# Buffers handed to the most urgent tile, and one layer's split weights kept in DRAM, in a two-layer hybrid decoder step

## The chip, the cores and the metric

One core of one Trainium2 chip runs the whole program. The metric is the device time of one execution in microseconds; lower is better. Three timed runs of the kernel before are known, and one profiled execution, from which all rows below come.

## The reference, cut to what matters

A prompt of 2048 tokens and a group of 8 samples with one new token each (and 2048 cached ones) go through two layers that share their weights. The even layer joins a gated MLP (A) and a stick-breaking attention (B); the odd one joins a top-k attention (C) and a pooling mixer (D). Each layer has one projection of its input and one of its output.

```python
def even_mixer(x, past_kv, w_in, w_sp, b_sp):          # layer 0
    h = jnp.einsum('btd,de->bte', x, w_in)
    u, v, gate_a, q, k, vb, gate_b = _split(h, EVEN_SPLITS)
...
    return jnp.concatenate([out_a, out_b], axis=-1), new_kv, v

def odd_mixer(x, past_kv, past_kidx, pool_buf, w_in, rel_bias, w_grp, scale):   # layer 1
    h = jnp.einsum('btd,de->bte', x, w_in)
    q, kv, q_idx, k_idx, w_idx, gate_c, p, gate_d = _split(h, ODD_SPLITS)
...
    return jnp.concatenate([out_c, out_d], axis=-1), new_kv, k_idx, new_buf

def post_norm(x, h, w_o, g, b):
    return _layer_norm(DN_ALPHA * x + jnp.einsum('bte,ed->btd', h, w_o), g, b)
```

All of it is float32. Layer 1's weights are `w_in_odd` (the projection of `odd_mixer`) and `w_out[1]`.

## The kernel before

**Tiling.** The prompt is cut into four blocks of 512 tokens. For each block and layer there are stages: `p0` (input projection of layer 0), `mixer_b`, `o0` (output projection of layer 0), `p1a` and `p1b` (input projection of layer 1), the tiles of mixer C (`c_tiles`: 16 query tiles of 128 tokens, with a top-k selection for each), and `o1`. The samples run as a stream beside them (`sample0`, `sample1`). The program interleaves up to three streams (`par`).

**Weights.** A projection multiplies in two parts: a value is split into a rounded part (`hi`, dtype float32r) and the rest (`lo`), and three products are added (xh·wh, xl·wh, xh·wl; lines 735 to 737, and 1132 to 1134 for the output projection). Weights come in pieces of 128 x 1024 numbers, 512 KB. `load_w` (line 656) brings each by a DMA on SP's queue into a tile `wr` (two buffers), ScalarE copies it into `wh` (line 661), and two VectorE subtractions of 512 columns make `wl` (line 664). `wh` and `wl` have two buffers each. Weights are read anew for every block: layer 1's input weights are 20 pieces, used by four blocks; its output weights are 8 pieces, used by four blocks, four of them once more for the last 128 rows (`out_tail`).

**Buffers.** SBUF tiles `tmp` (short-lived results) and `ot` (input and output of a block) have four buffers each; PSUM has two banks each of `pp` (projections), `pz` (the logits `z` of mixer B, `z_c` and `z_i` of C) and `pt` (transposes). VectorE or ScalarE must have read a bank before TensorE may fill it again.

**What sets the order.** The class `Order` plans each engine's instruction order before the program is built: `plan` goes through time with estimated costs, takes on each engine the ready instruction with the earliest latest-start (`latest`), and `settle` keeps the order with the shortest replay. `keep` fixes that order. In `plan`, tiles of one kind get their buffers strictly in the order in which the program names them (`queue[g].pop()` inside `take`), and the next one is served only after the first instruction of the one before it has started (`open_`).

**A branch in each selection.** `topk` ends with a check on VectorE and a conditional block (line 1595, `tc.If`); it is entered 14 times, and every engine's order is cut there.

Of the kernel before, what the change touches and what calls it, by code (L numbers as in the profile page):

```python
# [11 lines left out]
F32 = mybir.dt.float32  # L12
F32R = mybir.dt.float32r
# [9 lines left out]
P = 128  # L23
# [60 lines left out]


class Order:
# [4 lines left out]
    TILED, STAY, PATIENT = 150, 500, 40e3  # L91
    GUESSES = ((1.0, 200), (1.0, 250), (1.04, 230))
    ROUNDS, DRAWS, SPREAD = 5, 2, 0.05
# [48 lines left out]
    def gather(self):  # L142
# [83 lines left out]
        for t in sorted(self.uses, key=lambda t: self.uses[t][0]):  # L226
            if self.tiles[t].space != DRAM:
                self.tags.setdefault(self.tiles[t].tag, []).append(t)


# [86 lines left out]

    def settle(self):

        N, eng = len(self.ins), self.eng  # L320
        self.costs = [self.cost(n) for n in range(N)]
        for g, ms in self.group.items():
            busy = sum(self.costs[m][0] for m in ms)
            self.costs[g] = busy, busy + 170
        self.dma = [e is not None and "DMA" in i.opcode for e, i in zip(eng, self.ins)]
        self.kinds = [self.kind(n) for n in range(N)]
        self.ports = [self.port(n) for n in range(N)]
        self.succ = [[] for _ in range(N)]
        for n, d in enumerate(self.dep):
            for m in d:  # L330
                self.succ[m].append(n)
        self.links()
        draws, mid, best = [self.draw(k) for k in range(self.DRAWS)], self.costs, None
        sem = self.SEM
        for by, near in self.GUESSES:
            self.costs = [(b * by, l * by) if e in self.TAIL else (b, l) for e, (b, l) in zip(eng, mid)]
            self.SEM = near
            self.plan(list(range(N)))
            for _ in range(self.ROUNDS):
                self.SEM = near  # L340
                self.plan(self.latest())
                self.SEM = sem
                x = sum(self.replay(c) for c in draws)
                if best is None or x < best[0]:
                    best = x, self.order, self.after
        self.costs, (_, self.order, self.after) = mid, best

# [77 lines left out]
    def turns(self):  # L425
# [12 lines left out]
        return out  # L438

    def plan(self, rank):  # L440

# [9 lines left out]
        queue = {g: ts[::-1] for g, ts in self.tags.items()}  # L451
        free = {g: max(self.tiles[t].tag_meta.bufs for t in ts) for g, ts in self.tags.items()}
        open_ = dict.fromkeys(queue, True)
        users = {t: len(u) for t, u in self.uses.items()}
        self.after, gone = {}, {g: [] for g in queue}
        since, done, self.begun = [0.0] * N, [0.0] * N, [0.0] * N
# [11 lines left out]
        def take(g, t):  # L468
            while queue[g] and free[g] and open_[g]:
                x = queue[g].pop()  # L470
                if gone[g]:
                    self.after[x] = gone[g].pop(0)
                free[g] -= 1
                open_[g] = False
                for n in self.uses[x]:
                    release(n, t)
# [6 lines left out]
        while count < N:  # L483
            while back and back[0][0] <= now:
                _, g, x = pop(back)
                free[g] += 1
                gone[g].append(x)
                take(g, now)
# [9 lines left out]
            for e, q in ready.items():  # L498
                while q and idle[e] <= now:
# [42 lines left out]
                    for t in tiles[n]:  # L542
                        g, u = home[t], self.uses[t]
                        if n == u[0]:
                            open_[g] = True
# [67 lines left out]

    def keep(self):
        info = mybir.DependencyInfo(mybir.DependencyClass.NoSync, mybir.DependencyReason.DATA)
# [9 lines left out]
class Body:  # L625
    def __init__(self, ctx, tc, I, O):
        self.ctx, self.tc, self.nc, self.I, self.O = ctx, tc, tc.nc, I, O
        pool = lambda n, b, **k: ctx.enter_context(tc.tile_pool(name=n, bufs=b, **k))
        self.cst = pool("cst", 1)
# [25 lines left out]

    def load_w(self, src, shape, pool, bufs=2):
        nc = self.nc
        raw = self.loc.tile(shape, F32, tag="wr", name="wr", bufs=self.bufs["wr"])
        nc.sync.dma_start(raw, src)
        hi, lo = (pool.tile(shape, F32R, tag=n, name=n, bufs=bufs) for n in ("wh", "wl"))  # L660
        nc.scalar.copy(hi, raw)  # L661
        h = shape[1] // 2
        for e, c in ((nc.vector, slice(0, h)), (nc.vector, slice(h, 2 * h))):
            e.tensor_tensor(lo[:, c], raw[:, c], hi[:, c].bitcast(F32), op=OP.subtract)  # L664
        return hi, lo

    def rsqrt(self, out, var, eps, n):
# [9 lines left out]
        for _ in range(3):  # L677
# [3 lines left out]
            v.tensor_tensor(out, out, t[:n], op=OP.mult)  # L681

    def ps(self, name, shape=(P, TB)):

        b = next(b for b in BANKS.get(name, "pt").split() if b in self.banks)
        return self.banks[b].tile(list(shape), F32, tag=b, name=name)

    def tmp(self, name):
        return self.loc.tile([P, TB], F32, tag="tmp", name=name, bufs=self.bufs["tmp"])

# [124 lines left out]
    def plan_w(self, stages):  # L815

        I = self.I
        self.wplan, self.wready = [], []
        for st in stages:
            if st[:3] == "out":  # L820
                w = I["w_out"][int(st[3])]
                self.wplan += [(w[hf * 512:(hf + 1) * 512, cg * 256:(cg + 1) * 256], [P, 4, 256])
                               for cg in range(4) for hf in HALVES[int(st[3])]]
                continue
# [4 lines left out]
            w = I["w_in_even" if st == "p0" else "w_in_odd"][0]  # L829
            self.wplan += [(w[:, c:c + n], [P, KT, n]) for c, n in cols]  # L830
        for _ in range(2):
            self.more_w()

    def more_w(self, pool=None):
        if self.wplan:
            src, shape = self.wplan.pop(0)
            src = src.rearrange("(kt p) n -> p kt n", p=P)
            self.wready.append(self.load_w(src, shape, *((pool, 4) if pool else (self.wp,))))

# [247 lines left out]
    def otile(self, name):  # L1087
        return self.loc.tile([P, TB], F32, tag="ot", name=name, bufs=self.bufs["ot"])

# [1374 lines left out]

def build(nc, shapes):
    I = {n: nc.dram_tensor(n, s, d, kind="ExternalInput").ap() for n, s, d in shapes}
    O = {n: nc.dram_tensor("out_" + n, s, F32, kind="ExternalOutput").ap() for n, s in _OUTS}
    with tile.TileContext(nc, schedule_with_timeline_sim=True) as tc:
        with ExitStack() as ctx:
            body = Body(ctx, tc, I, O)  # L2470
            body.run()
        order = Order(tc, body.lags)
        order.gather()
        order.settle()
        order.keep()

# [12 lines left out]
```

## Time and profile before

| | us |
|---|---|
| median of 3 runs | 2790.44 |
| lowest, highest | 2785.44, 2792.58 |
| the profiled execution | 2784.49 |
| its span, first to last instruction | 2782.8 |
| TensorE busy in the span | 2672.8 |

The profiled execution took 1.7 us more than its span, and it is 6 us under the median. The profile lists, for each engine, the time in which an instruction of it was running. Matmuls overlap in TensorE's pipeline, and a running one that waits inside the pipeline counts as busy, so that TensorE's busy time holds stalls too; the distance from start to start tells them. PEld is TensorE's loading of its stationary operand. PEclk is the granted share of TensorE's clock.

### The profile page before, as it was taken

The page shows a single profiled execution, that of the slowest core. Times are in us where ns is not written, and L with a number is a line of the kernel's source. Part 1 is how long each engine was busy: PE and PEld are TensorE (multiplying, and loading weights), DVE is VectorE, ACT ScalarE, POOL GpSimd, SP SyncE. Part 2 cuts the span into 40 slices and gives each one's busy share as a digit, 9 for nine tenths or more (in the row PEclk, how much of TensorE's full clock was granted, in tenths as well). Part 3 has the DMA queues.
Part 4 walks back from the last instruction along what each step waited for, and adds up shares of the span by engine and source line. Part 5 has one row for each costly group of instructions (what it writes and reads, how often), then busy time and mean ns, then how long its engine had stood idle before and what let it go on. Part 6 is the DMA issues. An engine that isn't in the chain of part 4 may idle for free. (4 is left out here: it accounts for less than half of the span.)

```text
span 2782.8 us, 52464 instructions
## 1 busy us (share of the span) xinstructions
PE 2672.8 (96%) x17490; PEld 2154.5 (77%) x17490; DVE 2060.9 (74%) x5557; ACT 1604.3 (58%) x3216; POOL 766.3 (28%) x1040
## 2 busy tenths in 40 slices
PE   9999999999999999989899999999999999899996
PEld 7888787777777887768677677778777889898985
DVE  3466568775857886747988888897898788888865
ACT  3434333444444354435657677786686788688854
POOL 0111112210202321033433522334411445344222
PEclk9999999999999999999999999999999999999998
DMA  8666857895777777563764545433675666767462
GB/s 251 168 186 207 266 169 245 242 302 161 224 213 205 222 207 249 181 178 116 211 199 132 166 131 157 127 102 115 190 220 149 199 192 200 221 200 235 125 197 81
DMA packets 538914, 524.58 MB, mean 189 GB/s; under 512 B 43447, under 2 KB 411224, under 8 KB 538607
## 3 DMA queue, kind: packets, MB, share of 16 engines
q1 hardware_dynamic: 528759, 485.34, 58.9%
q0 software_dynamic: 9856, 35.66, 4.1%
q8 instruction: 139, 2.28, 0.3%
q14 instruction: 160, 1.31, 0.1%
HBM read 431.33 MB, written 89.73 MB: 187 GB/s over the span
## 5 line engine op out<-in xcount | busy, mean ns | idle before, releaser
L735 PE MATMUL pp<-xh,wh 128*128 128x512 f32 (+1 forms) x1536 | 624.0, 408 | 2.5 <-ACT wh L661 1.6
L736 PE MATMUL pp<-xl,wh 128*128 128x512 f32 (+1 forms) x1536 | 615.4, 401 | 0.0
L737 PE MATMUL pp<-xh,wl 128*128 128x512 f32 (+1 forms) x1536 | 613.6, 400 | 0.0
L664 DVE TENSOR_TENSOR wl<-wr,wh 128x512 fp32r<-128x512 f32 x520 | 354.5, 699 | 161.7 <-ACT wh L661 146.8
L661 ACT CAST wh<-wr 128x1024 fp32r<-128x1024 f32 x260 | 270.2, 1040 | 321.4 <-PE pp L736 160.2
L735 PEld LDWEIGHTS pp<-xh,wh 128*128 128x128 f32 (+1 forms) x1536 | 287.6, 188 | 67.4 <-issue 8.5
L737 PEld LDWEIGHTS pp<-xh,wl 128*128 128x128 f32 (+1 forms) x1536 | 287.6, 187 | 61.5 <-issue 4.4
L736 PEld LDWEIGHTS pp<-xl,wh 128*128 128x128 f32 (+1 forms) x1536 | 288.2, 188 | 53.9 <-issue 5.3
L1132 PE MATMUL pp_o<-wh,oh 128*128 128x256 f32 x1008 | 294.2, 294 | 5.4 <-DVE xres L1137 3.6
L1133 PE MATMUL pp_o<-wl,oh 128*128 128x256 f32 x1008 | 290.5, 289 | 0.2 <-DVE wl L664 0.2
L1134 PE MATMUL pp_o<-wh,ol 128*128 128x256 f32 x1008 | 288.5, 289 | 0.0
L1065 ACT COPY P<-ps_p 128x512 f32<-128x512 f32 (+2 forms) x320 | 166.5, 524 | 178.3 <-PE ps_p L1064 156.2
L1041 DVE TENSOR_TENSOR_SCAN P<-P,bfst 128x512 f32<-128x512 f32 x192 | 250.0, 1317 | 14.5 <-ACT P L1034 7.6
L1763 PE MATMUL z_c<-ksc,qc 128*128 128x512 f32 (+3 forms) x816 | 221.3, 356 | 22.9 <-DVE mx L1765 13.1
L1781 ACT ACTIVATE zt<-zt,nmax 128x512 f32<-128x512 f32 (+3 forms) x320 | 209.6, 657 | 54.1 <-DVE nmax L1769 52.2
L1750 POOL TENSOR_TENSOR nm<-nm,mk 128x256 f32<-128x256 f32 (+1 forms) x128 | 98.4, 770 | 420.2 <-DMA nm<-bft 161.3
L1796 ACT COPY zt<-ps_pc 128x512 f32<-128x512 f32 (+3 forms) x320 | 163.8, 522 | 81.6 <-PE ps_pc L1794 79.2
L1027 PE MATMUL z<-ks,q 128*128 128x512 f32 (+3 forms) x640 | 195.0, 390 | 13.1 <-DVE mx L1765 5.1
L1132 PEld LDWEIGHTS pp_o<-wh,oh 128*128 128x128 f32 x1008 | 193.3, 192 | 12.6 <-DVE xres L1137 4.6
L1133 PEld LDWEIGHTS pp_o<-wl,oh 128*128 128x128 f32 x1008 | 194.3, 193 | 4.1 <-issue 1.1
L1134 PEld LDWEIGHTS pp_o<-wh,ol 128*128 128x128 f32 x1008 | 193.4, 193 | 4.5 <-issue 2.2
L1509 ACT ACTIVATE mk<-ix,tk_tn 128x1152 int8<-128x1152 f32 (+13 forms) x140 | 183.8, 1313 | 17.7 <-DVE tk_tn L1559 6.6
(455 smaller groups left out, 5518.0 us busy)
## 6 DMA issues: line engine op xcount, KB each, us to landing
pg<-cache_b_kv SPq DMA_DIRECT2D x256, 256.0 KB
wr<-w_in_even SPq DMA_DIRECT2D x112, 512.0 KB
wr<-w_in_odd SPq DMA_DIRECT2D x76, 512.0 KB
wr<-w_out SPq DMA_DIRECT2D x68, 512.0 KB
ks<-ksc SPq DMA_DIRECT2D x80, 256.0 KB
ksc<-kcs SPq DMA_DIRECT2D x80, 256.0 KB
q<-qsc SPq DMA_DIRECT2D x64, 256.0 KB
qc<-qcs SPq DMA_DIRECT2D x128, 128.0 KB
```

The lines of the kernel that those rows point to most:

```text
L661: nc.scalar.copy(hi, raw)
L664: e.tensor_tensor(lo[:, c], raw[:, c], hi[:, c].bitcast(F32), op=OP.subtract)
L735: nc.tensor.matmul(ps[:m], wh[:, kt, :m], xh[kt], start=a, stop=False)
L736: nc.tensor.matmul(ps[:m], wh[:, kt, :m], xl[kt], start=False, stop=False)
L737: nc.tensor.matmul(ps[:m], wl[:, kt, :m], xh[kt], start=False, stop=b)
L1027: nc.tensor.matmul(z[:, :n], q2[:, c, t * P:(t + 1) * P].bitcast(F32R), ks[:, :n].bitcast(F32R), start=c == 0, stop=c == 1)
L1041: nc.vector.tensor_tensor_scan(r, r, r, initial=ini, op0=OP.mult, op1=OP.bypass)
L1132: nc.tensor.matmul(ps[:, :256], oh[:, tt], wh[:, k], start=a, stop=False)
L1133: nc.tensor.matmul(ps[:, :256], oh[:, tt], wl[:, k], start=False, stop=False)
L1134: nc.tensor.matmul(ps[:, :256], ol[:, tt], wh[:, k], start=False, stop=b)
L1763: nc.tensor.matmul(z[:, :n], q2[:, c, jj % 2, :].bitcast(F32R), kk, start=c == 0, stop=c == 1)
L1781: nc.scalar.activation(zt, zt, AF.Exp, bias=nmx, accum_out=st["rs"][:, h, c:c + 1])
```

## The change

It has two parts, and both alter the order that the planner writes.

**Buffers by urgency (`FREELY`).** For the kinds `ot`, `tmp`, `pt`, `pz` and `pp`, a free buffer goes to the most urgent waiting tile (by the planner's rank, among the first 8) instead of the next in program order, if `safe` finds that the tiles left can still be served in order. Which buffer each tile gets is planned too, so the kernel is built twice: the first build raises `Planned` with the order, the second takes the buffers from it (`turn`).

**Kept weights (`KEEP`).** For the first block in each of `p1a`, `p1b` and `out1`, the two parts `wh` and `wl` are written to DRAM after the split, 28 pieces in all, two DMAs each. For later blocks `load_w` reads both parts back, straight into `wh` and `wl`, with no ScalarE or VectorE work: 60 pieces of input weights and 28 of output weights. Every third of these (`THIRD`), outside `out_tail`, takes both buffers of `wr` in place of `wh` and `wl`.

```diff
+THIRD = True
+KEEP = {"p1a": 0, "p1b": 0, "out1": 0}
+FREELY = ('ot', 'tmp', 'pt', 'pz', 'pp')
...
+    def choose(self, queue, urgent, free, held, pending, any_):
+
+        least = queue[0]
+        if pending and (not any_ or self.span[pending][0] < self.span[least][0]):
+            return None
+        for x in urgent[:self.WINDOW] if any_ and not pending else ():
+            first = self.span[x][0]
+            if x != least and first > self.span[least][0] + self.AHEAD:
+                continue
+            for _, b in sorted(((held[b][0], b) for b in free if held[b][0] < first), reverse=True):
+                if self.safe(queue, held, x, b):
+                    return x, b
...
         def take(g, t):
-            while queue[g] and free[g] and open_[g]:
-                x = queue[g].pop()
...
+            while queue[g] and free[g]:
+                x = self.choose(queue[g], urgent[g], free[g], held[g], open_[g], g in self.free)
...
-    def load_w(self, src, shape, pool, bufs=2):
+    def load_w(self, src, shape, key, pool=None):
         nc = self.nc
-        raw = self.loc.tile(shape, F32, tag="wr", name="wr", bufs=self.bufs["wr"])
+        wr = lambda d, n: self.loc.tile(shape, d, tag="wr", name=n, bufs=self.bufs["wr"])
+        new = lambda d, n: (pool or self.wp).tile(shape, d, tag=n, name=n, bufs=4 if pool else 2)
+        kept = self.kept_w.get(key[::2])
+        if kept:
+            self.n_kept += 1
+            f = wr if THIRD and not pool and self.n_kept % 3 == 0 else new
+            hi, lo = f(F32R, "wh"), f(F32R, "wl")
+            for t, d in zip((hi, lo), kept):
+                nc.sync.dma_start(t.bitcast(F32), d)
+            return hi, lo
...
+        if KEEP.get(key[0]) == key[1]:
...
+            for t, d in zip((hi, lo), kept):
+                nc.sync.dma_start(d, t.bitcast(F32))
         return hi, lo
```

**TensorE at a branch.** The order of TensorE before, from the fourth selection's branch in the stage that runs `p1b(1)` beside tiles 2 to 5 of mixer C. `z` and `z_c` are tiles in the two `pz` banks, `av` and `av_c` are value products, `ps_pc` a transposition.

```order
L1595 UNCONDITIONAL_BRANCH
L1763 MATMUL z_c<-ksc,qc 128x384 x2
L737 MATMUL pp<-xh,wl 128x512
L735 MATMUL pp<-xh,wh 128x512
L736 MATMUL pp<-xl,wh 128x512
L737 MATMUL pp<-xh,wl 128x512
L1763 MATMUL z_c<-ksc,qc 128x128 x2
L735 MATMUL pp<-xh,wh 128x512
L1794 MATMUL ps_pc<-idf,zt 128x128 x4
L1027 MATMUL z<-ks,q_19848 128x384 x2
```

The same place in the order of the changed kernel (its lines stand some 90 further down).

```order
L1686 UNCONDITIONAL_BRANCH
L1854 MATMUL z_c<-ksc,qc 128x256 x2
L1118 MATMUL z<-ks,q_19871 128x128 x2
L1164 MATMUL av<-P,vs 64x512 x4
L826 MATMUL pp<-xl,wh 128x512
L1885 MATMUL ps_pc<-idf,zt 128x128 x4
L827 MATMUL pp<-xh,wl 128x512
L825 MATMUL pp<-xh,wh 128x512
L1118 MATMUL z<-ks,q_19871 128x256 x2
L1885 MATMUL ps_pc<-idf,zt 128x128 x3
L1854 MATMUL z_c<-ksc,qc 128x384 x2
```

In the order before, the third `pz` tile after the branch (`z` of 384 columns) comes behind two `z_c` tiles, five matmuls of `pp` and four transposes. Now the third one (`z` of 256 columns) comes behind a `z_c`, a `z`, four `av` products, three matmuls of `pp` and four transposes; the `z_c` here is named later in the program than the `z` that follows it.

**SP's queue while block 0 is in `p1b`.** Before: loads of weights (`wr`), of a page of the samples' cache (`pg`), and of mixer B's operands.

```order
L1020 DMA ks_11071<-ksc1_3_240 128x512
L1348 DMA qcs0_124<-q_hl_10257 128x1x512
L2003 TENSOR_LOAD pg_189
L659 DMA wr_10975<-w_in_odd 128x8x128
L2003 ISA x2
L659 DMA wr_11086<-w_in_odd 128x8x128
L659 DMA wr_11210<-w_in_odd 128x8x128
L1056 DMA vs_11093<-vsc1_1_266 128x512
L2012 ISA
L2012 DMA pg_11028<-cache_b_kv 128x512
```

After, at the same weights: each piece's two parts go out (`wh_p1b...<-wh`, `wl_p1b...<-wl`) around the load of the next one.

```order
L744 DMA wh_p1b_1572_10826<-wh_10821 128x1024
L1479 DMA dwg_11361<-d_w_grp 128x128
L735 DMA wr_11043<-w_in_odd 128x8x128
L744 DMA wl_p1b_1572_10827<-wl_10822 128x1024
L1111 DMA ks_11375<-ksc0_2_231 128x512
L744 DMA wh_p1b_2212_10938<-wh_10933 128x1024
L735 DMA wr_11158<-w_in_odd 128x8x128
L744 DMA wl_p1b_2212_10939<-wl_10934 128x1024
L1492 DMA otd1_0_97<-mx_10949 128x512
L744 DMA wh_p1b_1700_11050<-wh_11045 128x1024
```

Of ten rows here five are stores of 512 KB that were not there.

**SP's queue while block 1 is in `p1b`.** Before, one load per piece, into `wr`; `ksc`, `qc`, `nm` and `qi` are operands of mixer C.

```order
L659 DMA wr_18446<-w_in_odd 128x8x128
L1371 DMA gcd1_160<-gc_18291 128x512
L659 DMA wr_18637<-w_in_odd 128x8x128
L1020 DMA ks_18528<-ksc0_2_231 128x512
L1747 DMA qc_18346<-qcs0_124 64x4x128 x2
L1749 DMA nm_18266<-bft_2851 128x256
L1749 DMA nm_18349<-bft_2851 128x256
L1445 DMA qi_19173<-qis1_141 32x4x128 x4
L1371 DMA gcd1_160<-gc_18471 128x512
L659 DMA wr_19059<-w_in_odd 128x8x128
```

After, at two of the same pieces, two loads each, into `wh` and `wl`.

```order
L732 DMA wh_18678<-wh_p1b_1444_10676 128x1024
L732 DMA wl_18679<-wl_p1b_1444_10677 128x1024
L1840 DMA nm_18393<-bft_2851 128x256
L1462 DMA gcd1_160<-gc_18512 128x512
L1536 DMA qi_19208<-qis1_141 32x4x128 x4
L1838 DMA qc_18627<-qcs0_124 64x4x128 x2
L1833 DMA ksc_19077<-kcs0_0_128 128x512
L1840 DMA nm_18539<-bft_2851 128x256
L732 DMA wh_19097<-wh_p1b_2084_10747 128x1024
L732 DMA wl_19098<-wl_p1b_2084_10748 128x1024
```

The pair of loads of a piece stands in a row, ahead of operands of mixer C.

## Rows read from the trace of the kernel before

**Rows 1.** The page's first part: each engine's busy time, its share of the span, and its instructions.

```profile
PE 2672.8 (96%) x17490; PEld 2154.5 (77%) x17490; DVE 2060.9 (74%) x5557; ACT 1604.3 (58%) x3216; POOL 766.3 (28%) x1040
```

**Rows 2.** Busy time in three stretches of the span: up to 1240 us, from there to the end of the dense work, and the rest. Columns: length; busy us of PE, PEld, DVE, ACT and POOL with instructions; PEclk; DMA share; GB/s.

```profile
0.00:1240.00 1240.00, 1221.81 (x6845) 957.42 (x6846) 811.74 (x1491) 524.37 (x970) 213.72 (x336) 1.00 0.72 215
1240.00:2752.00 1512.00, 1445.47 (x10604) 1191.84 (x10603) 1232.64 (x4019) 1072.54 (x2236) 538.89 (x695) 0.98 0.57 168
2752.00:2782.79 30.79, 5.49 (x46) 5.28 (x44) 16.52 (x49) 7.38 (x10) 13.65 (x10) 0.67 0.42 138
```

**Rows 3.** TensorE's groups of one shape from 1240 to 2752 us, some of the costliest: count, then busy us, mean ns of one, and idle before them with what ended it.

```profile
L1132 PE MATMUL pp_o<-wh,oh 128*128 128x256 f32 x733 | 213.9, 294 | 3.3 <-DVE xres L1137 2.6 <-DVE fq L1586 0.6
L1133 PE MATMUL pp_o<-wl,oh 128*128 128x256 f32 x734 | 212.0, 290 | 0.2 <-DVE wl L664 0.2
L1134 PE MATMUL pp_o<-wh,ol 128*128 128x256 f32 x734 | 210.0, 289 | 0.0
L735 PE MATMUL pp<-xh,wh 128*128 128x512 f32 x456 | 187.6, 411 | 0.1
L736 PE MATMUL pp<-xl,wh 128*128 128x512 f32 x456 | 186.6, 409 | 0.0
L737 PE MATMUL pp<-xh,wl 128*128 128x512 f32 x456 | 186.1, 408 | 0.0
L1794 PE MATMUL ps_pc<-idf,zt 128*128 128x128 f32 x1088 | 182.0, 279 | 2.0 <-ACT zt L1796 0.7 <-ACT P L1065 0.7 <-ACT s16o L1148 0.4
L1808 PE MATMUL av_c<-zt,vsc 128*64 128x128 f32 x2176 | 153.0, 282 | 0.1
L1763 PE MATMUL z_c<-ksc,qc 128*128 128x512 f32 x336 | 118.2, 431 | 8.3 <-DVE mx L1765 4.1 <-DVE mx L1399 2.0 <-DVE P L1041 1.8
L1064 PE MATMUL ps_p<-idf,P 128*128 128x128 f32 x464 | 77.1, 277 | 5.8 <-ACT P L1065 4.6 <-DVE hT L762 1.0
L1027 PE MATMUL z<-ks,q 128*128 128x512 f32 x208 | 74.2, 431 | 1.1 <-ACT P L1031 0.6 <-ACT r L1456 0.5
```

**Rows 4.** The timeline of TensorE where nothing holds it: seven matmuls of `pp` lie between the first two rows.

```profile
153.94 0.39 PE L736 MATMUL pp<-xl,wh 128*128 128x512 f32 x1
...
155.78 0.39 PE L735 MATMUL pp<-xh,wh 128*128 128x512 f32 x1
```

**Rows 5.** The same view near the end: `pp_o` (five matmuls of it between the first two rows), then eight transposes and 48 value products.

```profile
2738.54 0.28 PE L1134 MATMUL pp_o<-wh,ol 128*128 128x256 f32 x1
...
2739.25 0.28 PE L1134 MATMUL pp_o<-wh,ol 128*128 128x256 f32 x1
...
2743.86 1.03 PE L1794 MATMUL ps_pc<-idf,zt 128*128 128x128 f32 x8
...
2744.83 2.84 PE L1808 MATMUL av_c<-zt,vsc 128*64 128x128 f32 x48
```

**Rows 6.** The same view in the middle: eight passes of `av`.

```profile
1551.52 1.94 PE L1073 MATMUL av<-P,vs 128*64 128x512 f32 x8
```

**Rows 7.** Who TensorE waited for from 1240 to 2752 us: us in total, times, longest.

```profile
PE z_c L1763 <- DVE mx L1765: 13.1, 8, 3.6
PE ps_so L2304 <- DMA s_pg<-cache_c_kv,s_rq: 7.0, 4, 2.4
...
PE z L1027 <- DVE mx L1765: 5.1, 1, 5.1
PE ps_p L1064 <- ACT P L1065: 4.6, 4, 1.9
```

**Rows 8.** The timeline around the branch of the first order shown above: DVEq is VectorE's sequencer.

```profile
1557.80 1.01 DVE L1511 TENSOR_SCALAR_CACHE_REDUCE mk<-ix,tk_tn 128x768 int8<-128x768 f32 x1 [3.63 <-DVEq L1595]
...
1561.87 0.56 DVE L1765 CUSTOM_DVE_ANT_0 zt<-z_c,mk 128x384 f32<-128x384 f32 x1 [3.05 <-issue]
...
1562.49 1.01 PE L1027 MATMUL z<-ks,q 128*128 128x384 f32 x2 [5.11 <-DVE mx L1765]
```

**Rows 9.** ScalarE's copies that make `wh`, from 1240 to 2752 us.

```profile
L661 ACT CAST wh<-wr 128x1024 fp32r<-128x1024 f32 x107 | 112.1, 1049 | 69.7 <-PE pp L736 31.1 <-PE pp_o L1134 25.9 <-PE ps_smp L753 4.7
```

**Rows 10.** VectorE's subtractions that make `wl`, in the same stretch.

```profile
L664 DVE TENSOR_TENSOR wl<-wr,wh 128x512 fp32r<-128x512 f32 x214 | 150.0, 713 | 24.0 <-ACT wh L661 16.0 <-DVEq L1595 6.2 <-PE ps_sk L2254 1.2
```

**Rows 11.** DMA issues of the whole span: layer 1's input weights, the output weights of both layers, and the small first piece of `p1a`.

```profile
wr<-w_in_odd SPq DMA_DIRECT2D x76, 512.0 KB
wr<-w_out SPq DMA_DIRECT2D x68, 512.0 KB
...
wr<-w_in_odd SPq DMA_DIRECT2D x4, 144.0 KB
```

**Rows 12.** Three stretches of 100 us before 1240, columns as in rows 2; block 0 is in `p1a` and `p1b` in the last two.

```profile
500.00:600.00 100.00, 100.00 (x536) 75.99 (x535) 73.40 (x137) 48.36 (x84) 19.53 (x21) 1.00 0.87 273
700.00:800.00 100.00, 99.76 (x536) 74.87 (x529) 74.07 (x117) 45.83 (x87) 14.86 (x27) 1.00 0.73 215
800.00:900.00 100.00, 100.00 (x495) 72.68 (x494) 69.46 (x113) 40.03 (x70) 13.05 (x28) 1.00 0.73 215
```

**Rows 13.** Whom SP's queue waited for before it could issue a load of weights, whole span.

```profile
SPq L659 <- DVE wl L664: 367.5, 152, 11.5
```

**Rows 14.** The timeline of the last microseconds: the issue of the last load of the layer norm's scale (`lng`), and a multiplication of the last rows by the scale.

```profile
2768.05 0.69 SPq L1210 DMA_DIRECT2D lng<-ln_g  x1
...
2772.91 1.26 POOL L1215 TENSOR_TENSOR xres<-xres,lng 128x512 f32<-128x512 f32 x1 [5.03 <-DMA lng<-ln_g]
```

More of the change, by code (lines that the diff above doesn't have):

```diff
@@ L83 @@
 }
+FREELY = ('ot', 'tmp', 'pt', 'pz', 'pp')
+class Planned(Exception):
+    pass
 class Order:
@@ L228, in gather @@
                 self.tags.setdefault(self.tiles[t].tag, []).append(t)
+        last = lambda n: max(self.group.get(n, (n,)))
+        self.span = {t: (u[0], max(map(last, u))) for t, u in self.uses.items()}
+        self.free = {g for g, ts in self.tags.items() if g.split("_")[0] in FREELY}
     def cost(self, n):
@@ L332, in settle @@
         self.links()
+        if plan:
+            self.order, self.after = plan[:2]
+            return
         draws, mid, best = [self.draw(k) for k in range(self.DRAWS)], self.costs, None
@@ L344, in settle @@
                 if best is None or x < best[0]:
-                    best = x, self.order, self.after
-        self.costs, (_, self.order, self.after) = mid, best
+                    best = x, self.order, self.after, self.slot
+        self.costs, (_, self.order, self.after, self.slot) = mid, best
     def draw(self, seed):
@@ L468, in take @@
         def take(g, t):
-            while queue[g] and free[g] and open_[g]:
-                x = queue[g].pop()
[L471 to L474, printed above, removed]
+            while queue[g] and free[g]:
+                x = self.choose(queue[g], urgent[g], free[g], held[g], open_[g], g in self.free)
+                if x is None:
+                    return
+                x, b = x
+                queue[g].remove(x)
+                if urgent[g] is not queue[g]:
+                    urgent[g].remove(x)
+                free[g].remove(b)
+                self.slot[x] = b
+                if held[g][b][1]:
+                    self.after[x] = held[g][b][1]
+                held[g][b] = self.span[x][0], x
+                open_[g] = x
                 for n in self.uses[x]:
@@ L612, in latest, with keep @@
         return [-s - c[0] for s, c in zip(start, cost)]
-    def keep(self):
+    def keep(self, plan):
+        if not plan:
+            raise Planned(self.order, self.after, {g: [self.slot.get(t, 0) for t in ts] for g, ts in self.made.items()})
         info = mybir.DependencyInfo(mybir.DependencyClass.NoSync, mybir.DependencyReason.DATA)
@@ L1087, in otile @@
     def otile(self, name):
-        return self.loc.tile([P, TB], F32, tag="ot", name=name, bufs=self.bufs["ot"])
+        return self.turn(self.loc, [P, TB], "ot", name, bufs=self.bufs["ot"])
     def out_parts(self, i, layer, last):
@@ L2469, in build @@
         with ExitStack() as ctx:
-            body = Body(ctx, tc, I, O)
+            body = Body(ctx, tc, I, O, plan and plan[2])
             body.run()
@@ L2473, in build @@
         order.gather()
-        order.settle()
-        order.keep()
+        order.made = body.made
+        order.settle(plan)
+        order.keep(plan)
 def kernel(**inputs):
```

81 lines of the change are left out of this document (61 added, 20 removed).

## The prediction

> **What bounds the kernel now.** I read the page's busy times first [rows 1]: TensorE runs 2672.8 us of a span of 2782.8, VectorE 2060.9, ScalarE 1604.3. TensorE is the long engine, so the question is what holds it, and where. Three stretches tell the second part [rows 2]. Up to 1240 us TensorE stands for 18 us of 1240 (1.5%) while VectorE is busy 65.5% and ScalarE 42%. From 1240 to 2752 it stands for 66.5 us of 1512 (4.4%), with VectorE at 81.5% and ScalarE at 71%, and its clock is at 0.98 of full speed instead of 1.00. The last 31 us hold almost no matmul. The DMA engines are fuller in the first stretch (0.72) than in the second (0.57).
>
> Busy time hides stalls, so I worked out how much of the second stretch is work. The distance from start to start in packed rows is 0.23 us for 512 columns ((155.78 - 153.94) / 8) [rows 4], 0.118 us for 256 columns of `pp_o` (0.71 / 6), 0.107 us for a transpose ((1.03 - 0.28) / 7) and 0.059 us for a pass of `av_c` (2.84 / 48) [rows 5]. With the counts [rows 3]: `pp` 1368 x 0.23 = 315, `pp_o` 2201 x 0.118 = 260, transposes 1552 x 0.107 = 166, `av_c` 2176 x 0.059 = 128, `z` and `z_c` of 512 columns 544 x 0.23 = 125. That is 994 us for 7841 matmuls, 0.127 each; the other 2763 at the same mean are an estimated 350. Together 1344 us, so about **168 us of the 1512 are not work**, of which 66.5 show as idle.
>
> LDWEIGHTS is busy 77% where matmuls are busy 96% [rows 1]. The Trainium skill, Perfetto Trace Analysis, section Identifying the Most-Contended Engine, says that matmul busy time is a poor measure of how near a kernel is to its roofline, and LDWEIGHTS busy a good one. By the first the whole room would be 110 us, by the second 628; the pitches above lie between, and the sum rests on them alone.
>
> Of the waits that show in this stretch, the first by size are for VectorE to empty a logits bank (13.1 and 5.1 us), then a gather's DMA (7.0), then ScalarE (4.6) [rows 7]. One of 5.1 us has a cause that the change doesn't touch: VectorE stood 3.63 us for its sequencer at the branch and 3.05 us more, and `z` had to wait for a bank [rows 8]. There are 14 such branches.
>
> **The change, part by part.** *Splitting work that goes away.* Layer 1's pieces after the first block: of 76 + 4 loads of input weights three quarters, 57 of 512 KB and 3 small ones; of 68 loads of output weights 28, since layer 0 has 32 and the first block of layer 1 has 8 [rows 11]. ScalarE loses 85 x 1.049 = 89 us [rows 9], VectorE 170 x 0.713 = 121 us [rows 10] (the small pieces left out), nearly all in the second stretch. VectorE goes from 1232.6 to 1111 us there (73.5%), ScalarE from 1072.5 to 983 (65%). Neither engine is the long one, so this is worth only what TensorE's stalls shrink. The two stretches give a scale: between them VectorE differs by 16.0 points and TensorE's visible idle share by 2.9 points of 4.4. If VectorE's load makes that difference, 8.0 points take back half, 1.47 of 4.4, a third of 168: **56 us**. If ScalarE's load makes it, 5.9 of 28.6 points take back 0.6 of 4.4: **23 us**. The waits name VectorE more than ScalarE [rows 7], so I take 45, and keep 23 and 56 as ends.
>
> *Buffers by urgency.* The order shown at the branch gives the price of one place. Before, the third `pz` tile comes behind two `z_c`, five `pp` and four transposes, about 0.35 + 0.12 + 1.15 + 0.43 = 2.0 us of work; after, behind a `z_c`, a `z`, four `av` (eight passes, 1.94 us) [rows 6], three `pp` and four transposes, about 3.4. That is 1.4 us more to cover VectorE's pause; at 14 branches 20 us at most, and nothing where the order there did not gain. The other four kinds have no wait of note [rows 7]. I take 8, ends 0 and 20.
>
> *The tail.* The last rows' multiplication by `lng` waited 5.03 us for a load issued at 2768.05 [rows 14], because its `tmp` buffer was late. With `tmp` given by urgency this may be sooner: I take 3, ends 0 and 5.
>
> *Writing the parts.* Block 0's 19 large pieces make 38 stores of 0.524 MB, 19.9 MB, between about 700 and 900 us. There the DMA engines carry 215 GB/s at 0.73; at 500 to 600 us they carried 273 GB/s at 0.87 [rows 12], which scales to 314 when full. The room is (314 - 215) x 200 us = 19.8 MB, just what is added. If it fits, it costs nothing; if all of it came on the path, 19.9 MB / 314 GB/s = 63 us. The loads behind the stores in SP's queue (the next piece, pages, `ks`) are what would be late, and TensorE behind them. It is nearer to fitting, as TensorE shows no idle there [rows 12]: I take a cost of 7, ends 0 and 63. The 8 pieces of output weights (8.4 MB) fall in the second stretch with its 0.57.
>
> *Reading the parts.* 85 loads more of 0.524 MB are 44.6 MB in 1512 us, 30 GB/s on 168; the share goes from 0.57 to about 0.67, which is free by itself. What changes is when a piece can start: `wh` must be read to the end by TensorE before the DMA may write it, where before only the copy and the two subtractions (1.05 + 2 x 0.71 = 2.5 us) waited for that and `wr` was filled ahead. Two parts at 314 GB/s need 3.3 us: 0.8 us longer, 88 times, is 70 us if nothing covers it. Every third piece lands in `wr` ahead of time, and TensorE has other streams between two pieces. SP's queue waits at the load now for TensorE and not for VectorE (367.5 us of waits) [rows 13]; mixer C's operands stand behind it. I take 4, ends 0 and 70.
>
> The Trainium skill, DMA: Bandwidth & Descriptors, section Anatomy of one DMA, gives about 2.0 us plus bytes / 436e3 for one DMA, which would be an estimated 3.2 us for one part; it is fitted to GpSimd's path, no row here shows a landing time, and by it the upper end would be 88 x (3.2 + 1.2 - 2.5) = 167 us instead of 70.
>
> **Sum:** -45 - 8 - 3 + 7 + 4 = -45 us. The span would be 2738, the profiled execution 2784.5 - 45 = 2739.5. That execution is 6 us under the median of the runs, so against the median I forecast 2790.4 - 45 = **2745 us**.
>
> **The rivals.**
>
> *More than that, 2701 us.* Waiting for a shared engine may grow as busy / (1 - busy). VectorE's goes from 0.815 / 0.185 = 4.4 to 0.735 / 0.265 = 2.8, 37% less: 62 of 168 us. With 20 us from the banks, some 15 us from half of the clock's missing 0.02 x 1512, and 8 us of DMA cost: -89. For it: the waits are spread over many short ones. Against it: the branches stay.
>
> *No change, 2790 us.* TensorE's stalls come from chains (logits, maximum, exponent, transpose, product) and branches, whose length does not depend on load; then only 8 + 3 - 7 - 4 = 0 are left. For it: VectorE and ScalarE both have idle time, and TensorE waited for `wl` and `wh` hardly ever [rows 3]. Against it: the first stretch has chains too and stalls a third as much. The Trainium skill, Perfetto Trace Analysis, section Identifying Performance Opportunities, says that improving a kernel means improving its most-contended engine; by that rule, with TensorE in that place, this is where relief of the others ends.
>
> *Slower, 2827 us.* The stores overfill the DMA queues. They decide from the point at which the demand at 700 to 900 us passes 314 GB/s; the sum above sits on that point, and the stores come in clumps (five in ten rows of SP's queue). Then up to 63 us come on the path in the first stretch, and the second gives only its lower end: +63 - 23 - 3 = +37. Against it: TensorE stood still for at most 0.2 us of each 100 there [rows 12], so loads had time in hand.
>
> *The change does not do what it says, 2756 us.* If the urgent tile is nearly always the next in the program's order, the first part is nothing: -45 + 7 + 4 = -34.
>
> **How the numbers follow.** Forecast 0.45, more 0.22, no change 0.13, slower 0.13, without the first part 0.07. The forecast's own range is 2709 (-56 - 20 - 5) to about 2785. The range given, **2688 to 2805**, takes in the deeper case with some room and the case of no change, with half of a clash of the stores; it leaves out most of the slower case and a little of the deeper one. A measurement of this kernel tells a change of 0.3% (8 us) from none. Faster than that: 0.45 + 0.22 + 0.07 = 0.74, less 0.01 at the forecast's edge: 0.73. Within 0.3%: 0.13. Slower: 0.14.
>
> **What would show it.** In the changed kernel's profile I expect, from about 1240 us to the end of the dense work, VectorE near 73% and ScalarE near 65%, TensorE's visible idle near 45 us, and that stretch some 50 us shorter. The first `wh` of a piece should show no DMA wait at TensorE beyond a few us in total. Around 700 to 900 us the DMA share should be near 1.0 with TensorE still at 99 to 100; if TensorE falls there, the slower case holds. If VectorE falls to 73% and TensorE's idle stays at 66 us, the relief was worth nothing, and the scale between the stretches was wrong.

## The result, and the profile after

The changed kernel takes 2754.14 us (median of four runs, 2748.54 to 2767.44) against 2789.86 for the kernel before: a ratio of 0.988, interval 0.9843 to 0.9918, or 23 to 44 us less. The forecast was 2745. The profiled execution took 2753.51 us with a span of 2751.5; before it was 2784.49 and 2782.8.

The windows, cut where the dense work now ends (2721 us, before 2752), columns as in [rows 2]:

```profile
0.00:1240.00 1240.00, 1222.55 (x6869) 958.74 (x6870) 820.76 (x1501) 526.66 (x979) 219.04 (x344) 1.00 0.77 233
1240.00:2721.00 1481.00, 1433.70 (x10582) 1187.84 (x10582) 1118.05 (x3835) 988.57 (x2140) 529.75 (x687) 0.98 0.65 206
2721.00:2751.50 30.50, 5.20 (x43) 4.99 (x42) 18.80 (x48) 7.27 (x10) 13.61 (x10) 0.64 0.42 139
```

In the second stretch VectorE is busy 75.5% (1118.05 / 1481) and ScalarE 66.8%, and TensorE's visible idle is 47 us: near the 73%, 65% and 45 us that the prediction named as its signs. The stretch is 31 us shorter, not some 50. The splitting that goes away is gone, too: in this stretch 22 copies and 44 subtractions are left of the 107 and 214 in [rows 9, 10] (the views by line).

```profile
L737 ACT CAST wh<-wr 128x1024 fp32r<-128x1024 f32 x22 | 23.0, 1048 | 25.1 <-PE pp_o L1225 21.8 <-issue 1.7 <-PE ps_so L1236 1.6
```

```profile
L740 DVE TENSOR_TENSOR wl<-wr,wh 128x512 fp32r<-128x512 f32 x44 | 31.9, 750 | 4.0 <-ACT wh L737 3.9
```

The stretches where block 0 writes its parts, beside the last two of [rows 12]: the DMA engines go up to a share of 0.98, and TensorE still runs for 99.26 us of 100.

```profile
700.00:800.00 100.00, 100.00 (x535) 76.79 (x535) 73.53 (x113) 47.30 (x88) 13.30 (x27) 1.00 0.89 279
800.00:900.00 100.00, 99.26 (x486) 73.88 (x485) 70.72 (x114) 40.45 (x72) 17.33 (x32) 1.00 0.98 326
```

Who TensorE waits for from 1240 to 2721 us, as in [rows 7]. The wait for VectorE to empty a bank before `z_c` fell by 1.6 us only; a kept `wh` is waited for once, 0.7 us.

```profile
PE z_c L1854 <- DVE mx L1856: 11.5, 9, 2.8
PE pp_o L1223 <- DVE xres L1228: 6.3, 4, 3.7
PE ps_pc L1885 <- ACT zt L1887: 5.6, 2, 5.4
PE ps_so L2395 <- DMA s_pg<-cache_c_kv,s_rq: 3.9, 4, 1.4
...
PE pp_o L1223 <- DMA wh<-wh_out: 0.7, 1, 0.7
```

The tail as in [rows 14] (from the timeline of GpSimd): the multiplication by `lng` still waits, now 5.38 us.

```profile
2742.20 2.48 POOL L1306 TENSOR_TENSOR xres<-xres,lng 128x512 f32<-128x512 f32 x2 [5.38 <-DMA lng<-ln_g]
```

From this profile alone the prediction's account looks confirmed: the relieved engines are at the level named, and the time came. Only a run of each part by itself tells that it is not so.

### The profile page after: what moved, and what is told of

It reads as the page before. It is cut to its first block, busy times and chain, and to the rows that moved or that the text cites. A ratio compares the mean times of both kernels' runs of the same rounds, so it can differ in the third digit from the quotient of the medians.

```text
span 2751.5 us, 52292 instructions
## 1 busy us (share of the span) xinstructions
PE 2661.4 (97%) x17490; PEld 2151.6 (78%) x17490; DVE 1957.6 (71%) x5381; ACT 1522.5 (55%) x3128; POOL 762.4 (28%) x1040
## 5 line engine op out<-in xcount | busy, mean ns | idle before, releaser
L825 PE MATMUL pp<-xh,wh 128*128 128x512 f32 x1536 | 622.9, 408 | 2.7 <-ACT wh L737 1.6
L826 PE MATMUL pp<-xl,wh 128*128 128x512 f32 x1536 | 616.0, 401 | 0.1
L827 PE MATMUL pp<-xh,wl 128*128 128x512 f32 x1536 | 612.7, 400 | 0.2 <-DMA otd<-c_sum 0.2
L825 PEld LDWEIGHTS pp<-xh,wh 128*128 128x128 f32 x1536 | 287.1, 187 | 69.3 <-issue 8.3
L737 ACT CAST wh<-wr 128x1024 fp32r<-128x1024 f32 x172 | 179.9, 1046 | 280.7 <-PE pp L826 138.7
L827 PEld LDWEIGHTS pp<-xh,wl 128*128 128x128 f32 x1536 | 287.2, 187 | 59.0 <-issue 3.9
L826 PEld LDWEIGHTS pp<-xl,wh 128*128 128x128 f32 x1536 | 287.8, 187 | 56.5 <-issue 8.1
L740 DVE TENSOR_TENSOR wl<-wr,wh 128x512 fp32r<-128x512 f32 x344 | 233.0, 701 | 123.3 <-ACT wh L737 118.7
L1600 ACT ACTIVATE mk<-ix,tk_tn 128x512 int8<-128x512 f32 (+13 forms) x140 | 183.4, 1310 | 32.5 <-DVE tk_tn L1650 14.5
L1856 DVE CUSTOM_DVE_ANT_0 zt<-z_c,mk 128x512 f32<-128x512 f32 (+3 forms) x256 | 148.2, 589 | 71.2 <-PE z_c L1854 37.7
```

The source lines that it names most:

```text
L825: nc.tensor.matmul(ps[:m], wh[:, kt, :m], xh[kt], start=a, stop=False)
L826: nc.tensor.matmul(ps[:m], wh[:, kt, :m], xl[kt], start=False, stop=False)
L827: nc.tensor.matmul(ps[:m], wl[:, kt, :m], xh[kt], start=False, stop=b)
L1600: nc.scalar.activation(mk.bitcast(I8)[:, :L], x, AF.Sign, bias=t3[:, c:c + 1], scale=-1.0, accum_out=ss[:, c // 2:c // 2 + 1])
```

## The experiments

Theory T is the prediction's: the relief of VectorE and ScalarE brings most of the gain. Rival U: the choice of buffers brings it. Rival S: every new order of the planner moves the time by as much, and the parts don't add up. All twelve kernels were timed in five rounds beside before, 5 to 12 executions each; gains in us are what the ratio lacks to 1, times 2783, the median of before beside these runs. The profile of each is one of these executions.

| kernel | median us | ratio to before (interval) | gain us |
|---|---|---|---|
| `free_only` | 2753.81 | 0.989 (0.9871 to 0.9909) | 31 |
| `keep_only` | 2786.41 | 1.0008 (0.9989 to 1.0027) | -2 |
| `seeds_after` | 2768.85 | 0.995 (0.9932 to 0.9968) | 14 |
| `seeds_before` | 2782.6 | 1.0001 (0.9988 to 1.0013) | 0 |
| `pz_only` | 2776.46 | 0.998 (0.9967 to 0.9993) | 6 |
| `no_pz` | 2765.5 | 0.9938 (0.9926 to 0.9951) | 17 |
| `relief` | 2791.63 | 1.0027 (1.001 to 1.0045) | -8 |
| `double_split` | 2803.71 | 1.008 (1.0067 to 1.0093) | -22 |
| `no_sub` | 2768.3 | 0.9938 (0.9915 to 0.9962) | 17 |
| `neither` | 2785.61 | 1.0004 (0.999 to 1.0019) | -1 |
| `sbuf_only` | 2762.23 | 0.9925 (0.9899 to 0.9951) | 21 |
| `free_other` | 2774.97 | 0.9964 (0.9947 to 0.9982) | 10 |

**The two parts alone.** `free_only`:

```diff
-KEEP = {"p1a": 0, "p1b": 0, "out1": 0}
+KEEP = {}
```

> Buffers by urgency alone; every piece of layer 1's weights is split anew for every block, as before. Theory T (the relief of VectorE and ScalarE brings most of the 36 us): about -8 us against before, 2775 to 2788, with VectorE busy as before (about 2061 us). Rival U (the choice of buffers brings most, since the last stage, which is relieved too, gained nothing): -25 us or more, 2755 to 2765, with VectorE's busy time unchanged. Rival S (each new order that the planner writes moves the time by some 15 us at random): any value, and then the parts do not add up.

`keep_only`:

```diff
-FREELY = ('ot', 'tmp', 'pt', 'pz', 'pp')
+FREELY = ()
```

> Kept weights alone; buffers are handed out in program order as before. Theory T: -25 to -35 us against before, 2755 to 2765, with VectorE near 1958 us and ScalarE near 1522 us busy. Rival U: 0 to -10 us, 2780 to 2790, though VectorE and ScalarE are relieved by the same 100 and 80 us. Rival S: any value; the gains of this kernel and of buffers by urgency alone then do not sum to 36 us.

Buffers by urgency alone give 31 us (25 to 36), as much as the whole change; kept weights alone give nothing. Theory T falls as it was stated, and rival U's ranges hold for `keep_only` and are missed by 1 us for `free_only`. The windows of the dense stretch show it, first of `keep_only`:

```profile
1240.00:2762.00 1522.00, 1450.51 (x10612) 1201.03 (x10611) 1137.96 (x3850) 991.68 (x2149) 521.19 (x695) 0.98 0.65 202
```

and of `free_only`:

```profile
1240.00:2726.00 1486.00, 1438.07 (x10600) 1191.14 (x10601) 1223.90 (x4017) 1069.00 (x2235) 548.25 (x690) 0.98 0.57 170
```

With the weights kept VectorE falls to 74.8% and ScalarE to 65.2%, and TensorE's idle is 71.5 us, against 66.5 in [rows 2]. With urgency VectorE stays at 82.4% and the idle falls to 47.9 us. So what the profile after shows of TensorE's idle time comes with urgency, and what it shows of VectorE and ScalarE with the kept weights.

**Other orders of the same work.** `seeds_after` and `seeds_before` change the draws by which the planner chooses among its orders; `free_other` keeps one of its three guesses of costs; `neither` switches both parts off in the changed code.

```diff
-        draws, mid, best = [self.draw(k) for k in range(self.DRAWS)], self.costs, None
+        draws, mid, best = [self.draw(k) for k in range(7, 7 + self.DRAWS)], self.costs, None
```

> The changed kernel, planned with two other random draws of the costs in the planner's replay (7 and 8 in place of 0 and 1): the same work, buffers and loads, another choice among the planned orders. Theory T and rival U: within 8 us of the changed kernel, 2746 to 2762. Rival S: off by 15 us or more.

> The kernel before, planned with the same two other draws: the same work and buffers, another choice among the planned orders. Theory T and rival U: within 8 us of before, 2782 to 2798. Rival S: off by 15 us or more, so that a part of the 36 us is the luck of one order.

```diff
 (free_only)
-    GUESSES = ((1.0, 200), (1.0, 250), (1.04, 230))
+    GUESSES = ((1.0, 250),)
```

> Buffers by urgency alone, all five kinds, but another of the planner's orders for them (the best under its second guess of costs only, where the first guess had the shortest replay). If urgency itself brings the gain: 2750 to 2766. If the gain was the luck of one order: 2770 to 2790.

```diff
-KEEP = {"p1a": 0, "p1b": 0, "out1": 0}
+KEEP = {}
-FREELY = ('ot', 'tmp', 'pt', 'pz', 'pp')
+FREELY = ()
```

> The changed code with both parts switched off, so that buffers are handed out in program order and weights are split anew. The planner's bookkeeping of buffers differs from before all the same, and it writes another order of the same work. If orders of one kind scatter little: within 8 us of before, 2775 to 2791. If a part of the gain comes from the bookkeeping and not from urgency: 2755 to 2772.

For the kernel before the other draws picked the same TensorE order (all 17490 products come in the same sequence in both traces), so `seeds_before` is only a repeat, and it repeats (1.0001). With urgency the order matters: 31 against 10 us without kept weights, 33 against 14 with them. `free_other` falls into the range that was named for the luck of one order, and `seeds_after` is off by 14.7 us, almost the 15 of rival S. So rival S is half right: the size of the gain is uncertain by some 20 us from order to order. Its sign isn't, as far as the runs go: all four kernels with five kinds by urgency are faster than before, and none of those that hand out buffers in program order and keep all the subtractions or the kept weights (`neither`, `keep_only`, `relief`) is.

**Which buffers.** `pz_only`, `no_pz` and `sbuf_only` are `free_only` with fewer kinds:

```diff
-FREELY = ('ot', 'tmp', 'pt', 'pz', 'pp')
+FREELY = ('pz',)                       # pz_only
+FREELY = ('ot', 'tmp', 'pt', 'pp')     # no_pz
+FREELY = ('ot', 'tmp')                 # sbuf_only
```

> Buffers by urgency for the logits banks (pz) alone, no kept weights. If the gain of buffers by urgency (28 us in the run with that part alone) is what I priced at 8 us, the logits banks at the branches and the waits for VectorE to empty them, then this alone gives it: 2752 to 2765. Rival: the gain comes from the projection banks, the transposes or the SBUF tiles, or needs several kinds together: 2775 to 2790.

> Buffers by urgency for ot, tmp, pt and pp, not for the logits banks; no kept weights. If the logits banks carry the gain: 2775 to 2790. If the other four do: 2750 to 2765. If each gives half: near 2769.

> Buffers by urgency for the SBUF kinds ot and tmp alone, no kept weights. The logits banks alone gave 6 us and the other four kinds 17. If ot and tmp carry these 17: 2762 to 2770. If the PSUM kinds pp and pt do: 2776 to 2788.

(The 28 us named in the first of these lie inside the interval of the 31 in the table.) The logits banks give 6 us, near the 8 that I had priced, and TensorE's waits for `mx` before `z_c` and `z`, 18.2 us in [rows 7], are 12.3 in `pz_only`. With all five kinds they are no shorter (18.1 in `free_only`), so it isn't by them that urgency gains its 31 us. The two SBUF kinds, of which I had said that they show no wait of note, give 21. With `pt` and `pp` added it is 17 (`no_pz`): these two add nothing that stands out from the scatter of orders, and by the same scatter the shares of the kinds are known to some 10 or 20 us only.

One place of that can be read. Near 1240 us an output projection of layer 0 begins, and its weights load while the operands of mixers B and C for the next stretch do. Here is before, first 100 us and then four times 10:

```profile
1200.00:1300.00 100.00, 89.90 (x543) 76.48 (x542) 60.26 (x138) 47.29 (x100) 40.09 (x59) 0.91 0.53 151
1230.00:1240.00 10.00, 7.57 (x57) 6.79 (x56) 4.99 (x11) 4.38 (x11) 7.39 (x8) 1.00 0.94 239
1240.00:1250.00 10.00, 5.04 (x43) 4.84 (x41) 2.63 (x6) 0.00 (x0) 2.64 (x7) 0.85 1.03 261
1250.00:1260.00 10.00, 7.74 (x23) 5.80 (x24) 6.28 (x17) 5.89 (x15) 4.97 (x11) 0.50 0.50 146
1260.00:1270.00 10.00, 9.55 (x60) 7.83 (x59) 6.55 (x13) 7.09 (x15) 2.93 (x7) 0.80 0.27 79
```

and `sbuf_only`:

```profile
1200.00:1300.00 100.00, 94.01 (x621) 80.37 (x620) 69.44 (x171) 50.90 (x113) 41.14 (x63) 0.97 0.59 165
1230.00:1240.00 10.00, 6.74 (x30) 5.75 (x30) 1.75 (x5) 3.73 (x8) 5.67 (x6) 0.66 0.86 267
1240.00:1250.00 10.00, 9.88 (x76) 9.12 (x75) 7.70 (x20) 5.93 (x14) 6.35 (x14) 1.00 0.73 203
1250.00:1260.00 10.00, 10.00 (x78) 9.14 (x76) 8.93 (x18) 7.37 (x18) 3.46 (x7) 1.00 0.55 169
```

In before TensorE stands for 10.1 us of these 100, 5.11 of them in one wait, and after it had stood for half of 1240 to 1250 its granted clock is 0.50 of full speed, the level of 1.2 GHz, for the next ten. The two levels show in the pitch of equal matmuls, in its timeline: 0.21 us apart at the low level, 0.12 soon after.

```profile
1261.91 0.41 PE L1145 MATMUL ps_so<-wh,osx 128*16 128x256 f32 x1
1262.12 0.41 PE L1145 MATMUL ps_so<-wl,osx 128*16 128x256 f32 x1
...
1264.17 0.28 PE L1145 MATMUL ps_so<-wl,osx 128*16 128x256 f32 x1
1264.29 0.28 PE L1145 MATMUL ps_so<-wh,osx 128*16 128x256 f32 x1
```

If every microsecond at the low level loses half of itself, the clock costs 0.09 x 100 = 9 us, and the place loses 19; in `sbuf_only` it is 6.0 + 3 = 9. What ends the longest wait in before is a load of `qi`, an operand of mixer C. The `qi` come in sets of four: a first set served a product at 1234.48, the one waited for is the second. SP's timeline tells why it is late, here of before, with TensorE's wait as the last row:

```profile
1214.62 5.81 SPq L659 DMA_DIRECT2D wr<-w_out  x2
...
1224.91 0.37 SPq L659 DMA_DIRECT2D wr<-w_out  x1
1226.02 2.80 SPq L1100 DMA_DIRECT2D ot<-otd  x3
1228.87 0.71 SPq L1155 DMA_DIRECT2D xs_res<-x_sample  x2
1229.76 0.36 SPq L1100 DMA_DIRECT2D ot<-otd  x1
1230.23 1.78 SPq L1445 DMA_DIRECT2D qi<-qis  x4
...
1244.07 1.88 SPq L1445 DMA_DIRECT2D qi<-qis  x4
...
1250.15 0.77 PE L1453 MATMUL z_i<-kid,qi 128*128 128x256 f32 x2 [5.11 <-DMA qi<-qis]
```

and of `sbuf_only`, also with TensorE's longest wait as the last row:

```profile
1207.85 5.81 SPq L735 DMA_DIRECT2D wr<-w_out  x2
1213.85 1.99 SPq L1536 DMA_DIRECT2D qi<-qis  x4
...
1227.55 1.48 SPq L1191 DMA_DIRECT2D ot<-otd  x2
1229.13 0.39 SPq L735 DMA_DIRECT2D wr<-w_out  x1
...
1231.72 3.19 SPq L1536 DMA_DIRECT2D qi<-qis  x4
...
1232.98 0.58 PE L1223 MATMUL pp_o<-wh,oh 128*128 128x256 f32 x1 [4.46 <-ACT oh L714]
```

In program order the loads into `ot` and `tmp` (`xs_res`) are issued ahead of mixer C's first operand and behind a third `wr` load, and the issues of `wr` loads wait for the subtractions (five waits, 23.0 us in all, between 1195 and 1250 us). Everything behind them moves: the first set of `qi` goes out at 1230.23, and the second at 1244.07, behind nearly 14 us of other issues. With urgency the first set goes out right behind the two `wr` loads, 16 us earlier, and the second 12 us earlier, so that no product waits for it. Of these 16 us some 7 are a lead that `sbuf_only` already had at the two `wr` loads (1207.85 against 1214.62). The price is that the `ot` loads come later: TensorE now waits 4.46 us for `oh`, which is made from them, and the clock of that window is 0.66, where before has 0.85, 0.50 and 0.80 in three windows.

The runs split without exception: the first `qi` is issued at 1212 to 1221 us and the clock of the 100 us is 0.97 in all six kernels with `ot` and `tmp` by urgency, at 1227 to 1236 us and 0.91 to 0.93 in all eight others, before among them. The idle time of the 100 us does not split so (10.05 us in `seeds_after`, 6.5 in `pz_only`), as other waits fall into them. A better measure of the place is how far a kernel is ahead of before: the start of its n-th `z` product less that of the n-th in before, as the median over those within 25 us. From 1150 to 1275 us the six gain 7 to 10 us by it, and the eight others between -1 and 3. In `sbuf_only` the lead is 5 us at 1150, 14 at 1275, 15 at 1500, 21 at 1700, 16 at 2000 and 23 at 2600 (the last two by `z_c`). So this place gives some 8 to 10 of the 21 us, and the rest comes before 1150 and after 1500. I could not pin that rest to places, and `neither`, which gains nothing in the end, is 3 us ahead at 1150 and 10 at 1700.

**What the relief is worth.** `relief` is `keep_only` with one part, which alone is written and read; `no_sub` and `double_split` load as before and take away, or double, the subtractions of later blocks. The diffs are cut.

```diff
 (keep_only)
-            hi, lo = f(F32R, "wh"), f(F32R, "wl")
-            for t, d in zip((hi, lo), kept):
-                nc.sync.dma_start(t.bitcast(F32), d)
-            return hi, lo
+            hi = f(F32R, "wh")
+            nc.sync.dma_start(hi.bitcast(F32), kept[0])
+            return hi, hi
...
```

> Kept weights without buffers by urgency, with one part only: the first block writes wh and later blocks read wh alone and use it for both parts (the low part of these weights is left out of the sums, matmuls are as many). So VectorE and ScalarE are relieved as in the changed kernel, with the DMA traffic of reading as before and half of the writing. If the relief is worth something and the traffic of the two parts eats it: faster than before by 15 us or more, 2755 to 2768. If the relief itself is worth nothing (what keeping the weights alone gave): 2778 to 2790.

```diff
 (neither)
-        hi, lo = new(F32R, "wh"), new(F32R, "wl")
+        hi = new(F32R, "wh")
         nc.scalar.copy(hi, raw)
+        if key[0] in ("p1a", "p1b", "out1") and key[1] != 0:
+            return hi, hi
+        lo = new(F32R, "wl")
         h = shape[1] // 2
```

> The kernel before with VectorE alone relieved: for later blocks of layer 1 the piece is loaded and copied to wh as before, the two subtractions are left out and wh is used for both parts (the low part of these weights is missing from the sums; matmuls are as many). VectorE loses the same 121 us as by the kept weights; loads, their place in the queue, wr and ScalarE's copy stay. If the relief of VectorE brings 23 to 56 us and the kept weights lost it again by loads that start late: 2735 to 2760. If the relief is worth nothing: 2774 to 2790.

```diff
 (neither)
+        twice = 2 if key[0] in ("p1a", "p1b", "out1") and key[1] != 0 else 1
-        for e, c in ((nc.vector, slice(0, h)), (nc.vector, slice(h, 2 * h))):
+        for e, c in ((nc.vector, slice(0, h)), (nc.vector, slice(h, 2 * h))) * twice:
```

> The kernel before with more VectorE work: for later blocks of layer 1 each subtraction that makes wl runs twice, 170 subtractions of 0.713 us more, 121 us, in the places that the kept weights relieve. If VectorE's load sets TensorE's stalls by the scale of the prediction (8 points of load for 23 to 56 us): 2805 to 2840. If the load is worth nothing on this side either: 2780 to 2792.

The engines' busy times of `no_sub` and `double_split`, as in [rows 1]:

```profile
PE 2655.6 (96%) x17490; PEld 2147.3 (78%) x17490; DVE 1969.3 (71%) x5381; ACT 1601.6 (58%) x3216; POOL 766.8 (28%) x1040
PE 2679.6 (96%) x17490; PEld 2157.4 (77%) x17490; DVE 2143.0 (77%) x5733; ACT 1601.3 (57%) x3216; POOL 783.6 (28%) x1040
```

Of the 121 us that were expected VectorE's busy time falls by 92 in the one (176 instructions fewer) and grows by 82 in the other. It has a price, by these runs: 92 us less gain 17 (11 to 24), 82 us more cost 22 (19 to 26). Both times lie between the two ranges that were named. So theory T may have a true core, of 17 where it took 45. Two things keep this from being shown: each is one order only, and orders with urgency scatter by 20 us (the four in program order that gain nothing, before, `neither`, `keep_only` and `relief`, lie within 8); and without the subtractions a `wr` buffer is free sooner, so the loads of the next pieces can start sooner too.

The kept weights don't collect that price, and not because of their reading traffic: `relief` reads as many bytes as before and is no faster. The profiles offer one lead, the granted clock. Mean clock and span give the time lost to the low level as span x (1 - clock), an estimate that counts all of it as lost, and in every row some 10 us of it lie in the last 31 us, where there is almost no matmul. The means over all executions of each kernel:

| | span | clock | lost us | span less that |
|---|---|---|---|---|
| before (65 beside these runs) | 2782.5 | 0.981 | 52 | 2731 |
| `neither` | 2784.1 | 0.982 | 50 | 2734 |
| `keep_only` | 2784.8 | 0.981 | 53 | 2732 |
| `relief` | 2790.4 | 0.979 | 58 | 2733 |
| `no_sub` | 2766.5 | 0.985 | 42 | 2724 |
| `double_split` | 2801.6 | 0.980 | 55 | 2746 |
| `sbuf_only` | 2762.7 | 0.987 | 37 | 2725 |
| `free_only` | 2751.7 | 0.987 | 36 | 2716 |
| after | 2754.1 | 0.985 | 42 | 2712 |
| `seeds_after` | 2768.3 | 0.982 | 49 | 2719 |

By it 15 of the 24 us between `relief` and `no_sub` are clock, and what VectorE's relief gives at full clock is 7 to 10 us without urgency, and perhaps 4 with it (`free_only` to after, which the times of 0.989 and 0.988 don't tell apart). Of the 31 us of `free_only`, too, half is clock. That does not make the clock a cause by itself: at 1240 us it fell after TensorE had waited.

Where the kept weights fall behind can be read. By the n-th `z_c`, `relief` is 8 us behind `no_sub` at 1500 us, 9 at 2000 and 27 at 2600; `keep_only` is 3, 10 and 18 behind. From 2000 to 2700 us the windows are, of `no_sub`, `relief` and `keep_only`:

```profile
2000.00:2700.00 700.00, 670.24 (x5372) 585.86 (x5372) 515.36 (x1814) 527.83 (x1044) 242.68 (x268) 0.99 0.63 192
2000.00:2700.00 700.00, 665.08 (x5203) 578.82 (x5203) 512.00 (x1808) 487.72 (x992) 257.74 (x280) 0.97 0.64 199
2000.00:2700.00 700.00, 666.21 (x5234) 580.96 (x5234) 521.94 (x1830) 490.52 (x1006) 246.22 (x280) 0.97 0.73 237
```

There 14 us are clock by the estimate (0.02 x 700), and 4 to 5 more are idle time. Whether the clock is low with kept weights because of how they land (straight in `wh` and `wl`, once TensorE has read the last piece), or by the luck of these orders, stays open: a second order of `no_sub` and `keep_only`, and parts that land in `wr` first, would tell it, and were not tried.

## Why the prediction came out near, and where it was wrong

The time was right to 9 us; its reasons were not, and that the sum came out near is luck.

- **Relief, -45 (23 to 56): wrong.** It was forecast to bring -34 with the costs of the kept weights (-45 + 7 + 4); measured it is 0 (`keep_only`, -3 to +8 us on the time). The step that failed is the scale between two stretches: it took the difference in TensorE's idle share between the stages for an effect of VectorE's load, when the stages also differ in their streams, their branches and in places as that at 1240 us. `keep_only` has VectorE at 74.8% and TensorE's idle at 71.5 us, where the scale wanted about 45. `no_sub` puts the load's price at 17 us (11 to 24), in one order and where the loads stay. The rule of the Trainium skill that I had weighed as a rival (Perfetto Trace Analysis, Identifying Performance Opportunities: improve the most-contended engine) is nearer to these runs than my scale, though the 17 and 22 us for VectorE, busy 81.5% of the second stretch in [rows 2], suggest that it isn't the whole of it.
- **Buffers by urgency, -8 (0 to 20): too small.** 31 us in the order of `free_only`, 10 in that of `free_other`. The price for the logits banks held in the run with these alone (6 us, 2 to 9). What failed is "the other four kinds have no wait of note": I looked for their waits at TensorE, but in program order the loads into `ot` and `tmp` stand ahead of another mixer's operand in SP's queue, and the wait for that operand has a DMA's name.
- **The tail, -3: nothing.** The wait for `lng` is 5.38 us instead of 5.03, and the span ends 25.6 us after the start of the last `pp_o` product in both (2757.2 and 2725.9).
- **Writing, +7 (0 to 63): near the lower end.** The stores went through at 326 GB/s, 0.98 of the DMA engines, with TensorE at 99.26 of 100 us at the least. Up to 1200 us `keep_only` has started 6642 products, before 6650.
- **Reading, +4 (0 to 70): open.** A `wh` was waited for 0.7 us, so the direct price is nothing. But what `no_sub` gains the kept weights don't, and if that isn't the luck of orders, their landing costs about as much, 18 to 24 us.
- **The rivals.** "No change" gave the right number for the kept weights, but its reason, stalls that don't depend on load, has `no_sub` and `double_split` against it; its terms for the buffers were too small. "More than that" fell: `keep_only` took VectorE to 74.8% and gained nothing. "Slower" fell, since the stores fitted. "Doesn't do what it says" fell: if the urgent tile were nearly always the next one, `free_only` could not gain 31 us.
- **The signs.** VectorE near 73%, idle near 45 us and a stretch some 50 us shorter were to show the relief at work. The first comes with the kept weights and the second with urgency, which brings idle to 47.9 us with VectorE at 82.4%; together they could not tell the one cause from the other. The last sentence of that part names the right test, VectorE down and idle unchanged; it is what `keep_only` shows.

So the kept weights were forecast at -34 and gave 0, the buffers and the tail at -11 and gave -31 in this order: two errors of 34 and 20 us with opposite signs. In the order of `seeds_after` the same change takes 2768.85 us, 24 more than the forecast.

## What to carry to other kernels

When two edits come in one change, a profile of both can show every sign that one of them was to give; run each alone before crediting it. A load into a buffer that is handed out in program order need not show as a wait for that buffer: look on the DMA-issuing queue at what stands behind it. Where a planner rewrites the whole order, time a second order of the same work, since here two orders differed by some 20 us, more than most edits.

## What the hardware showed that was not expected

The granted clock of TensorE, as a mean over a kernel's executions, differed from 0.979 (`relief`) to 0.987 (`free_only`) between kernels of almost the same work, by the estimate above 58 to 36 us of the span; the difference is two thirds of the whole gain. It differs as much within one kernel: of the twelve executions of `keep_only`, the shortest span is 2773.1 us at 0.984 and the longest 2800.4 at 0.976, and by the estimate 23 of these 27 us are clock. At 1240 us it fell to 0.50 after a stretch in which TensorE was busy 5.04 of 10 us. And 16 DMA engines at a share of 0.98 moved 326 GB/s, more than the 314 that I had scaled from 0.87, while TensorE stood for 0.74 us of those 100.
